# A Strassen-type matmul with GELU: opening in half chunks, block sums put behind the next operand sums, GELU table loaded in front

## Chip, cores, metric

One core of one Trainium2 chip. The metric is device time in microseconds (us) of one execution; the median of several runs is quoted. The runs are compared with runs of the kernel before on the same chip in the same rounds.

## The reference

```python
m, k, n = 4096, 4096, 4096                    # a, b: float32, normal
x = np.matmul(a, b)
return 0.5 * x * (1 + np.tanh(np.sqrt(2 / np.pi) * (x + 0.044715 * x**3)))
```

## The kernel before

The output is made in 16 blocks of 1024 x 1024. Each block takes seven products of half-size matrices instead of eight, with sums of operands (`aS`, `bS`) and sums of results, so 7/8 of the matmuls of a plain product. Operands are loaded as float32 and cast to float16 by the transfer (queue of GpSimd, POOL); A is then transposed by VectorE (DVE). A chunk is 512 x 1024 of A or 1024 x 512 of B, 1.05 MB as float16. The first block does its first half in depth by plain products, which need no sums and few chunks; its second half is done by the seven products, in half as many steps as later blocks have ("half steps"). In the code, X and Y (`accX`, `accY` in the profile) are the running sums of the products in the matmul engine's accumulators; `x1`, `x7` and `m5` are copies of X after three of the products (the prediction's M1 and M5 are among them); `c12` and `c21` are the plain parts of two quadrants of the first block. Near its end the kernel reads a verdict on the size of its inputs, which decides whether another, general path has to run as well; the wait near 1520 us belongs to it.

```python
PLAIN = [   # quadrant of the output, quadrant of A, quadrant of B
    ("12", "11", "12"), ("11", "11", "11"), ("12", "12", "22"), ("11", "12", "21"),
    ("21", "21", "11"), ("21", "22", "21"), ("22", "21", "12"), ("22", "22", "22"),
]
N_PLAIN = 2 * len(PLAIN)
N_WARM = 28                     # matmuls of zeros ahead of the first product
...
def turn_a(mb, quad, c):        # DVE; load_a issues 4 transfers of 256 KB, load_b 8 of 128 KB
    s = staged.pop((mb, quad, c))                 # "stage": two buffers
    t = pool.tile([P, NJ // 2, TM * 2], F16, name="aT", tag=f"aT{a_slot[quad]}{c}")
    ...
    nc.vector.transpose(dst, src)
...
def settle(gi, s, i):           # after the last step of product s, tile i of 4
    X, Y = banks.get(("X", i)), banks.get(("Y", i))
    if s == 1:
        m5 = keep("m5", X, 2)                     # copy on ScalarE (ACT)
        flush()                                   # GELU and output of what waits
        y = new_y()                               # four buffers in all
        tt(y, Y, m5, ALU.subtract)                # on DVE
        if gi == 0:
            tt(y, y, post.pop(("c12", i)), ALU.add)   # the plain part of the first block
        waiting.append((gi, i, 0, 1, y, y))
    elif s == 2:
        post["x7", i] = keep("x7", X, RT)
    elif s == 3:
        x1 = post["x1", i] = keep("x1", X, RT)
        x7 = post["x7", i]
        tt(x7, x1, x7, ALU.subtract)
        tt(x1, Y, x1, ALU.subtract)
        if gi == 0:
            tt(x1, x1, post.pop(("c21", i)), ALU.add)
    ...                         # s = 4: output from X;  s = 5: y = x1 - Y;  s = 6: y = Y + x7
...
for n, whats in (               # ahead of which step: L(oad) A, B and T(ranspose), quadrant_chunk
    (0, "A11_0 B12_0 T11_0 B11_0 A12_0"), (2, "B22_0"), (4, "T12_0 B21_0 A21_0 A22_0"),
    (8, "T21_0 B12_1 B22_1 A11_1"), (10, "T22_0 A12_1"), (14, "T11_1 A22_1 B21_1 B11_1"),
    (16, "T12_1 A21_1"), (18, "T22_1"), (24, "T21_1"),
): ...
for n, step in enumerate(steps):
    ...                         # loads and transposes of this step
    make_sums(...)              # operand sums of step n + 2, on DVE
    flush()
    plain(n) if step[1] < 0 else multiply(*step)
```

Every engine works through its own instructions in this order. What DVE has ahead of a transpose or an operand sum therefore delays it, even where the data are there.

## Time and profile before

| | |
|---|---|
| median of 3 runs | 1596.88 us (1596.72 to 1597.02) |
| span in the profile | 1595.7 us |

The prediction below shows where the time goes, with its lines. The wait for the transposed A21, in the timeline of DVE (start, duration, engine, line, operation, count):

```profile
45.67 0.69 DVE L366 TENSOR_TENSOR x<-x,accX 128x512 f32<-128x512 f32 x1 [0.18 <-PE accX L291]
46.27 4.50 DVE L151 STREAM_TRANSPOSE aT<-stage 128x2048 uint32<-128x2048 uint32 x2
```

The fourth of four additions that wait for PE stands ahead of the transpose, and PE goes on at 48.63 when the first of the two transposes is done.

### The profile page before, as it was taken

What the parts mean: (1) busy time and instruction counts of PE and PEld (TensorE: products, weight loads), DVE (VectorE), ACT (ScalarE), POOL (GpSimd) and SP (SyncE); (2) the same over time, 40 slices, a digit from 0 to 9 for tenths busy, and PEclk for the clock granted to TensorE, in tenths of its full rate; (3) what the DMA queues carried; (4) which work ended last, traced back from release to release, by engine and by line L of the source; (5) the groups of instructions that cost most, each with busy time, mean ns of one, the idle gap of its engine ahead of it and who ended that gap; (6) DMA issues with size and microseconds to landing.
All of it is one profiled execution on the core that took longest, in us unless ns stands there. A gap on an engine that the chain in (4) does not pass through costs nothing. (4 is left out here: it accounts for less than half of the span.)

```text
span 1595.7 us, 19619 instructions
## 1 busy us (share of the span) xinstructions
PE 1568.2 (98%) x7228; PEld 708.3 (44%) x7228; DVE 1229.6 (77%) x1365; ACT 522.5 (33%) x714; POOL 530.9 (33%) x964
## 2 busy tenths in 40 slices
PE   8999999999999999999999999999999999999988
PEld 3444444444444444444444444444444444444433
DVE  1398898867877888985778778887787779888674
ACT  0035545411121545531111344541212145454111
POOL 7563441440323144341124423245021443514300
PEclk9999999999999999999999999999999999999999
DMA  9997683890957578587497837689377786837702
GB/s 179 189 222 149 119 181 74 143 197 27 198 98 147 113 132 158 103 164 130 78 164 118 184 74 147 135 133 178 60 135 129 133 158 106 173 80 136 152 16 81
DMA packets 224792, 211.13 MB, mean 132 GB/s; under 512 B 19888, under 2 KB 191920, under 8 KB 224688
## 3 DMA queue, kind: packets, MB, share of 16 engines
q0 software_dynamic: 187392, 142.67, 60.8%
q1 hardware_dynamic: 37296, 67.13, 11.6%
q8 instruction: 59, 0.97, 0.2%
q14 instruction: 45, 0.37, 0.1%
HBM read 285.22 MB, written 67.11 MB: 221 GB/s over the span
## 5 line engine op out<-in xcount | busy, mean ns | idle before, releaser
L291 PEld LDWEIGHTS <-aS 128*128 128x128 f16 x4960 | 485.6, 98 | 595.9 <-DVE aS L264 7.0
L160 POOL DMA_DIRECT2D bR<-in_b_dram x832 | 448.8, 544 | 709.7 <-DVE bS L264 338.6
L264 DVE TENSOR_TENSOR aS<-aT 128x2048 f16<-128x2048 f16 x310 | 376.0, 1219 | 151.1 <-PE accX L291 117.4
L291 PE MATMUL accX<-bS,aS 128*128 128x512 f16 x1984 | 432.5, 380 | 4.3 <-DVE bS L264 4.1
L264 DVE TENSOR_TENSOR bS<-bR 128x2048 f16<-128x2048 f16 x310 | 375.5, 1218 | 52.5 <-PE accX L291 41.0
L291 PEld LDWEIGHTS <-aT 128*128 128x128 f16 x2240 | 219.6, 98 | 277.7 <-issue 12.4
L357 ACT ACTIVATE y<-y 128x512 f32<-128x512 f32 x192 | 118.7, 630 | 337.9 <-DVE y L366 337.7
L291 PE MATMUL accY<-bR,aS 128*128 128x512 f16 x992 | 216.7, 379 | 3.0 <-DVE aS L264 3.0
L291 PE MATMUL accY<-bS,aS 128*128 128x512 f16 x992 | 216.7, 379 | 1.6 <-DVE y L366 1.6
L291 PE MATMUL accX<-bS,aT 128*128 128x512 f16 x992 | 217.0, 379 | 0.0
L291 PE MATMUL accX<-bR,aS 128*128 128x512 f16 x992 | 216.7, 379 | 0.0
L291 PE MATMUL accY<-bS,aT 128*128 128x512 f16 x992 | 216.7, 379 | 0.0
L366 DVE TENSOR_TENSOR energy<-energy,square 128x1024 bf16<-128x1024 bf16 x240 | 164.6, 686 | 9.3 <-ACT square L185 5.4
L140 POOL DMA_DIRECT2D stage<-in_a_dram x128 | 81.9, 646 | 255.6 <-DVE aT L151 186.5
L344 ACT COPY x<-accX 128x512 f32<-128x512 f32 x128 | 75.1, 587 | 220.0 <-PE accX L291 220.0
L185 ACT ACTIVATE square<-aT 128x1024 bf16<-128x1024 f16 x120 | 123.8, 1051 | 64.9 <-DVE energy L366 64.6
L185 ACT ACTIVATE square<-bR 128x1024 bf16<-128x1024 f16 x120 | 123.5, 1051 | 58.1 <-DVE energy L366 57.4
L151 DVE STREAM_TRANSPOSE aT<-stage 128x2048 uint32<-128x2048 uint32 x32 | 73.7, 2305 | 47.8 <-DMA stage<-in_a_dram 47.8
L344 ACT COPY m<-accX 128x512 f32<-128x512 f32 x64 | 37.1, 580 | 214.4 <-PE accX L291 214.4
L366 DVE TENSOR_TENSOR x<-accX,x 128x512 f32<-128x512 f32 x64 | 43.9, 691 | 41.0 <-ACT y L357 41.0
L357 ACT ACTIVATE y<-accX 128x512 f32<-128x512 f32 x64 | 38.2, 597 | 112.7 <-PE accX L291 112.7
L291 PE MATMUL accY<-bR,aT 128*128 128x512 f16 x192 | 45.4, 398 | 9.7 <-DMA bR<-in_b_dram 6.6
(35 smaller groups left out, 307.9 us busy)
## 6 DMA issues: line engine op xcount, KB each, us to landing
bR<-in_b_dram POOLq DMA_DIRECT2D x832, 128.0 KB, 5.2
out_dram<-y SPq DMA_DIRECT2D x256, 256.0 KB, 5.6
stage<-in_a_dram POOLq DMA_DIRECT2D x128, 256.0 KB, 7.0
row<-seen_d SPq DMA_DIRECT2D x2, 1.5 KB, 3.0
seen_d<-seen SPq DMA_DIRECT2D x1, 3.0 KB, 7.7
```

The costliest lines, as they stand in the source:

```text
L140: nc.gpsimd.dma_start(out=s[g * Q : (g + 1) * Q, :, :], in_=a_v[kh * CH + c, g, :, x0 : x0 + TM // Q, :],)
L151: nc.vector.transpose(dst, src)
L160: nc.gpsimd.dma_start(out=t[g * Q : (g + 1) * Q, e::2, :], in_=b_v[kh * CH + c, g, e, :, :, n0 : n0 + NC],)
L185: nc.scalar.activation(t[:, :], src, ACT.Square)
L264: nc.vector.tensor_tensor(out=t[:, :], in0=part(tiles, blk, o[0], q), in1=part(tiles, blk, o[1], q), op=ALU.add if o[2] > 0 else ALU.subtract,
L291: nc.tensor.matmul(acc[:, :], sa[:, j // 2, i * P : (i + 1) * P, j % 2], sb[:, j, :], start=start and j == 0, stop=stop and j == 3, skip_g ...
L344: nc.scalar.copy(out=t[:, :], in_=src[:, :])
L357: nc.scalar.activation(y[:, :], src[:, :], ACT.Gelu_apprx_tanh)
L366: nc.vector.tensor_tensor(out=o[:, :], in0=x[:, :], in1=y[:, :], op=op)
```

## The change

The intent: begin products with half chunks; keep the matmul engine (PE) warm until then; take additions that nobody waits for out of the way of operand sums; load the GELU table where ACT is idle. Cut to its core:

```diff
-N_WARM = 28
+N_WARM = 44
 def load_a(mb, quad, c, h=None):          # h: half of the rows; 4 transfers of 128 KB each
 def turn_a(mb, quad, c, h=None):          # half a transpose
 def load_b(nb, quad, c, h=None):          # h: even or odd rows in depth
 def plain(n):                             # first four products by halves of B,
                                           # last four by halves of A's rows
 def flush():
     for args in waiting:
+        plain_part = post.pop((f"c{ih + 1}{jh + 1}", i), None) if gi == 0 else None
+        if plain_part is not None:
+            tt(y, y, plain_part, ALU.add)
         emit(*args)
+def combine():                            # called behind make_sums and flush of the next step
+    for gi, i in later:
+        x7, x1 = post["x7", i], post["x1", i]
+        tt(x7, x1, x7, ALU.subtract)
+        tt(x1, banks["Y", i], x1, ALU.subtract)
+    later.clear()
 # settle, s == 1 and s == 5:
-    flush()
+    if gi:
+        flush()
-    if gi == 0:
-        tt(y, y, post.pop(("c12", i)), ALU.add)
 # settle, s == 3:
-    tt(x7, x1, x7, ALU.subtract)
-    tt(x1, Y, x1, ALU.subtract)
-    if gi == 0:
-        tt(x1, x1, post.pop(("c21", i)), ALU.add)
+    later.append((gi, i))
 # loads:
-    (0, "A11_0 B12_0 T11_0 B11_0 A12_0"), (2, "B22_0"), (4, "T12_0 B21_0 A21_0 A22_0"),
+    (0, "A11_0 B12_0 T11_0 B11_0 A12_0 B22_0 B21_0 A21_0"), (4, "T12_0 A22_0"),
-    (24, "T21_1"),
+    (22, "T21_1"),
+table = pool.tile([P, 1], F32, name="table", tag="table")
+nc.vector.memset(table[:, :], 0.0)
+nc.scalar.activation(table[:, :], table[:, :], ACT.Gelu_apprx_tanh)
```

More of the change, by code (lines that the diff above doesn't have):

```diff
@@ L43 @@
 PLAIN = [
-    ("12", "11", "12"), ("11", "11", "11"), ("12", "12", "22"), ("11", "12", "21"),
-    ("21", "21", "11"), ("21", "22", "21"), ("22", "21", "12"), ("22", "22", "22"),
+    ("12", "11", "12", False), ("11", "11", "11", False), ("12", "12", "22", False), ("11", "12", "21", False),
+    ("21", "21", "11", True), ("21", "22", "21", True), ("22", "21", "12", True), ("22", "22", "22", True),
 ]
 N_PLAIN = 2 * len(PLAIN)
-N_WARM = 28
+N_WARM = 44
 SQUARE_MAX = 2.0**26
@@ L132, in half_path, with load_a, turn_a, load_b @@
     staged = {}
-    def load_a(mb, quad, c):
+    def load_a(mb, quad, c, h=None):
         ih, kh = int(quad[0]) - 1, int(quad[1]) - 1
-        x0 = (ih * MH + mb * TM) // Q
-        s = pool.tile([P, TM // Q, RUN], F16, name="stage", tag="stage", bufs=2)
+        n = NX if h is None else NX // 2
+        x = 0 if h is None else h * n
+        x0 = (ih * MH + mb * TM) // Q + x
+        if not h:
+            s = pool.tile([P, NX, RUN], F16, name="stage", tag="stage", bufs=2)
+            staged[mb, quad, c] = s
+        s = staged[mb, quad, c]
         for g in range(4):
             nc.gpsimd.dma_start(
-                out=s[g * Q : (g + 1) * Q, :, :],
-                in_=a_v[kh * CH + c, g, :, x0 : x0 + TM // Q, :],
-            )
-        staged[mb, quad, c] = s
-    def turn_a(mb, quad, c):
-        s = staged.pop((mb, quad, c))
-        t = pool.tile([P, NJ // 2, TM * 2], F16, name="aT", tag=f"aT{a_slot[quad]}{c}")
+                out=s[g * Q : (g + 1) * Q, x : x + n, :],
+                in_=a_v[kh * CH + c, g, :, x0 : x0 + n, :],
+            )
+    def turn_a(mb, quad, c, h=None):
+        if not h:
+            t = pool.tile([P, NJ // 2, TM * 2], F16, name="aT", tag=f"aT{a_slot[quad]}{c}")
+            a_tiles[mb, quad, c] = t
+        s, t = staged[mb, quad, c], a_tiles[mb, quad, c]
+        x = slice(0, NX) if h is None else slice(h * NX // 2, (h + 1) * NX // 2)
         src = s.bitcast(U32).rearrange("p mb (jj q) -> p jj mb q", q=Q)
         dst = t.bitcast(U32).rearrange("p jj (mb q) -> p jj mb q", q=Q)
-        nc.vector.transpose(dst, src)
-        a_tiles[mb, quad, c] = t
-    def load_b(nb, quad, c):
+        nc.vector.transpose(dst[:, :, x, :], src[:, :, x, :])
+        if h != 0:
+            del staged[mb, quad, c]
+    def load_b(nb, quad, c, h=None):
         kh, jh = int(quad[0]) - 1, int(quad[1]) - 1
         n0 = jh * NH + nb * NC
-        t = pool.tile([P, NJ, NC], F16, name="bR", tag=f"bR{b_slot[quad]}{c}")
-        for g in range(4):
-            for e in range(2):
+        if not h:
+            b_tiles[nb, quad, c] = pool.tile(
+                [P, NJ, NC], F16, name="bR", tag=f"bR{b_slot[quad]}{c}"
+            )
+        t = b_tiles[nb, quad, c]
+        for e in range(2) if h is None else (h,):
+            for g in range(4):
                 nc.gpsimd.dma_start(
@@ L163, in load_b @@
                 )
-        b_tiles[nb, quad, c] = t
     def part(tiles, blk, quad, q):
@@ L307, in plain @@
     def plain(n):
-        (quad, oa, ob), q = PLAIN[n // 2], n % 2
+        (quad, oa, ob, by_rows), h = PLAIN[n // 2], n % 2
         chain = "X" if quad == "11" else "Y"
         seen = [x for x in range(len(PLAIN)) if PLAIN[x][0] == quad]
-        start = n == 2 * seen[0]
-        stop = n == 2 * seen[-1] + 1
-        for i in range(RT):
+        sa, sb = a_tiles[0, oa, 0], b_tiles[0, ob, 0]
+        sa = sa.rearrange("p jj (m e) -> p jj m e", e=2)
+        tiles = [(j, e) for j in range(NJ // 2) for e in range(2) if by_rows or e == h]
+        for i in range(h * RT // 2, (h + 1) * RT // 2) if by_rows else range(RT):
             acc = banks[chain, i]
-            products(acc, part(a_tiles, 0, oa, q), part(b_tiles, 0, ob, q), i, start, stop)
+            start = n // 2 == seen[0] and (by_rows or h == 0)
+            stop = n // 2 == seen[-1] and (by_rows or h == 1)
+            for j, e in tiles:
+                nc.tensor.matmul(
+                    acc[:, :], sa[:, j, i * P : (i + 1) * P, e], sb[:, 2 * j + e, :],
+                    start=start and (j, e) == tiles[0], stop=stop and (j, e) == tiles[-1],
+                    skip_group_check=True,
+                )
             if not stop:
@@ L351, in flush @@
         for args in waiting:
+            gi, i, ih, jh, y, _ = args
+            plain_part = post.pop((f"c{ih + 1}{jh + 1}", i), None) if gi == 0 else None
+            if plain_part is not None:
+                tt(y, y, plain_part, ALU.add)
             emit(*args)
         waiting.clear()
+    later = []
+    def combine():
[4 more added lines that the diff above has]
+        later.clear()
     def emit(gi, i, ih, jh, y, src):
@@ L381, in settle @@
         elif s == 3:
-            x1 = post["x1", i] = keep("x1", X, RT)
-            x7 = post["x7", i]
-            tt(x7, x1, x7, ALU.subtract)
-            tt(x1, Y, x1, ALU.subtract)
-            if gi == 0:
-                tt(x1, x1, post.pop(("c21", i)), ALU.add)
+            post["x1", i] = keep("x1", X, RT)
+            later.append((gi, i))
         elif s == 4:
@@ L395, in settle @@
             tt(y, post.pop(("x1", i)), Y, ALU.subtract)
-            flush()
+            if gi:
+                flush()
             waiting.append((gi, i, 1, 0, y, y))
@@ L417, in half_path @@
     for n, whats in (
-        (0, "A11_0 B12_0 T11_0 B11_0 A12_0"),
-        (2, "B22_0"),
-        (4, "T12_0 B21_0 A21_0 A22_0"),
+        (0, "A11_0 B12_0 T11_0 B11_0 A12_0 B22_0 B21_0 A21_0"),
+        (4, "T12_0 A22_0"),
         (8, "T21_0 B12_1 B22_1 A11_1"),
@@ L429, in half_path @@
             fn = {"A": load_a, "B": load_b, "T": turn_a}[what[0]]
-            before.setdefault(n, []).append((fn, (0, what[1:3], int(what[4]))))
+            for h in (0, 1) if what[4] == "0" else (None,):
+                before.setdefault(n, []).append((fn, (0, what[1:3], int(what[4]), h)))
     nxt_b = {"12": "22", "22": "21", "21": "12", "11": "11"}
@@ L507, in half_path @@
             flush()
+            combine()
             if step[1] < 0:
```

## The prediction

> **What bounds the kernel now.** I read the page's totals first, then the busy times by stretch, then the matmul engine's timeline over the first 145 us, then the transfers of the first 60 us, then the waits after 1500 us.
>
> ```profile
> span 1595.7 us, 19619 instructions
> PE 1568.2 (98%) x7228; PEld 708.3 (44%) x7228; DVE 1229.6 (77%) x1365; ACT 522.5 (33%) x714; POOL 530.9 (33%) x964
> ```
>
> Of 7228 matmuls 28 are warm-up, so 7200 are work. The stretches say what one costs and where PE is not full:
>
> ```profile
> core 0: us, PE busy (x) PEld busy (x) DVE busy (x) ACT busy (x) POOL busy (x), PEclk, DMA share, GB/s
> 0.00:20.00 20.00, 12.54 (x42) 4.78 (x43) 2.58 (x2) 1.28 (x1) 14.65 (x29) 0.83 1.06 159
> 40.00:60.00 20.00, 16.93 (x71) 7.20 (x70) 7.17 (x6) 0.00 (x0) 12.74 (x23) 0.91 1.32 196
> 100.00:120.00 20.00, 17.00 (x80) 7.60 (x79) 18.61 (x23) 4.74 (x8) 13.54 (x25) 1.00 1.18 229
> 200.00:400.00 200.00, 200.00 (x928) 90.73 (x927) 159.79 (x184) 71.45 (x96) 58.78 (x107) 1.00 0.64 124
> 1500.00:1560.00 60.00, 55.90 (x253) 24.92 (x252) 38.72 (x55) 10.69 (x19) 0.00 (x0) 0.97 0.07 23
> ```
>
> 928 matmuls in 200 us is 0.2155 us each; 7200 of them are 1551.6 us. So 44 us of the span are lost, and no change that leaves the count alone can gain more. They lie at the two ends: between 140 and 1500 us PE is full. The timeline of PE shows the opening:
>
> ```profile
> 1.31 7.93 PE L303 MATMUL accX<-zeros 128*128 128x512 f16 x28 [1.31 <-DVE zeros L298]
> 15.37 8.69 PE L291 MATMUL accY<-bR,aT 128*128 128x512 f16 x32 [6.12 <-DMA bR<-in_b_dram]
> 31.18 0.38 PE L291 MATMUL accY<-bR,aT 128*128 128x512 f16 x1 [0.21 <-DMA bR<-in_b_dram]
> 38.49 7.07 PE L291 MATMUL accX<-bR,aT 128*128 128x512 f16 x32
> 48.63 29.49 PE L291 MATMUL accY<-bR,aT 128*128 128x512 f16 x128 [3.08 <-DVE aT L151]
> 94.72 11.38 PE L291 MATMUL accX<-bS,aS 128*128 128x512 f16 x52 [0.20 <-ACT m L344]
> 116.02 7.08 PE L291 MATMUL accY<-bR,aS 128*128 128x512 f16 x32 [3.00 <-DVE aS L264]
> 124.68 7.07 PE L291 MATMUL accY<-bS,aS 128*128 128x512 f16 x32 [1.58 <-DVE y L366]
> 131.58 13.76 PE L291 MATMUL accY<-bS,aT 128*128 128x512 f16 x63
> ```
>
> The first block of output ends at 131.58 us after 480 matmuls, 103.4 us of work: 28.1 us are lost. They are: 15.37 before the first product; 1.6 because the first 32 take 8.5 instead of 6.9 us (slow clock); 0.8 on both sides of 31.18; 3.2 before 48.63 and 1.7 of slow clock behind it; 0.4 before 94.72; 3.2 before 116.02; 1.8 before 124.68. At the other end 5.7 us go with the wait at 1524 us (verdict on the inputs, then slow clock) and 7.8 us are the tail after the last matmul. The change touches neither.
>
> The transfers decide what the opening can gain:
>
> ```profile
> DMA  0099999999999999999999999999999999999999
> GB/s 0 3 124 192 153 181 201 202 202 200 202 203 199 188 196 196 201 200 203 199 203 201 212 187 195 196 196 195 195 197 199 202 202 204 202 200 203 197 181 167
> ```
>
> Each slice is 1.5 us. The load queue runs at 200 GB/s without a pause from 8 us on: a chunk of 1.05 MB takes 5.3 us, half a chunk 2.6 us. Nothing in the opening can come sooner than this queue brings it, unless it waits for less of it.
>
> **What the Trainium skill says.** "TensorE: Matmul & The Clock Gate", section "What's actually happening": the array's clock is halved after about 3.4 us of idleness and comes back after as much activity. The trace agrees: after the idle 9.24 to 15.37 and before 48.63 the granted clock falls and matmuls follow each other at 0.43 instead of 0.2155 us; but 3.00 us of idleness before 116.02 cost no clock, so it depends on where the gap lies. "Perfetto Trace Analysis", section "DMA Optimizations": splitting transfers lets work start sooner if the engines are idle; here they are full, so a split buys only the finer granularity. "ScalarE: Activation LUTs", section "What ACT_TABLE_LOAD costs": about 1283 ns plus a drain per switch; the trace has two loads of 1.28 us, one at 0.86 us, one at 90.85 us ahead of the first GELU. "VectorE: DVE Perf Modes", section "The three transpose paths": the DVE transposes 32x32 blocks; here 2.31 us a chunk, so I take 1.15 us for half.
>
> **The change, part by part.** The order of instructions per engine shows that the sequence of chunks in the load queue is unchanged; only the pieces are halves, and the eight loads of a chunk may be the eight outstanding ones.
>
> 1. First product. It waits now for half of A, its transpose, and half of B: three halves ahead of it instead of four. Before, the fourth half let PE start at 15.37; 2.6 us earlier is 12.7. The warm-up, 44 instead of 28, ends at 9.24 + 16 x 0.2155 = 12.7. Both agree; I take 12.8. Gain 2.6, and with no idle gap the 1.6 us of slow clock too: **-4.2**.
>
> 2. Products 3 and 4 of the plain part. PE, 4.2 us ahead, runs out at 12.8 + 64 x 0.2155 = 26.6. The next needs half of B22, whose whole let PE go at 31.2, so its half is there at 28.6 (A12, transposed from 26.58 on, is ready by 27.8). Stall 2.0 where there were 0.8: **+1.2**. From here the queue is no longer ahead of PE by more than half a chunk.
>
> 3. A21. Before, DVE took up its transpose only behind the four additions that wait for PE: PE ended at 45.4, DVE began at 46.27, the transpose of 2.31 ended when PE went on at 48.63. It still stands there, but PE needs half of it: 0.9 + 1.15 = 2.1 us stall instead of 3.2, too short for the slow clock: **-2.8**. Then PE runs to the end of the plain part at 12.8 + 2.0 + 2.1 + 55.2 = 72.1, against 77.96: 5.9 us gained so far.
>
> 4. The half steps behind it (72 to 120 us). Here DVE is full (18.6 of 20 us), so its queue is the path. Per piece from the trace: transpose 2.3, operand sum 1.14, PSUM sum 0.6 to 0.7. Following the new order: T12, two sums, T22, four sums and the four y of M5 end at about 87.5; two sums; the four delayed additions of c12 end at 92.2; two sums; the last transpose runs 94.5 to 96.8 (its data land at 92.7); three sums to 100.2. So the sum before the sixth product is there at 100.2 and needed at 106.5: the 3.2 us wait vanishes, and the copy delayed by the table load (0.4) too: **-3.6**. The eight deferred M1 additions end at 105.5, before PE writes that bank again. But M5's GELUs now wait for the delayed c12, and the four copies behind them on ACT hold PE by some 0.8 us near 93: **+0.8**. DVE then has one sum, four additions, four sums before the y of the seventh product: ready at 114.4 with PE at 114.2; stall 0.2 instead of 1.8: **-1.6**.
>
> 5. The c21 additions go behind that y and the next sum, so GELU starts 3.5 us later relative to PE (118 instead of 114.5), output lands 5.2 to 7.5 us later, and its four buffers hold the next four y, which stand before an operand sum on DVE. Before, that sum was ready 1.9 us early (136.6 against 138.5); now some 1.6 us late: **+1.5**.
>
> 6. In the other 15 blocks the M1 sums move behind an operand sum. PE has no wait there to lose: 0. The table load itself lies beside work in both: 0 more.
>
> Sum: -4.2 + 1.2 - 2.8 - 3.6 + 0.8 - 1.6 + 1.5 = -8.7, so 1596.9 - 8.7 = 1588.2; I say **1588**.
>
> **Rivals.** (a) The load queue takes everything back: PE gets ahead and meets it at each chunk. For it: 200 GB/s without a pause, and step 2 is such a wait. Against: the chunks behind A22 were there before PE needed them by 5 us and more, as no wait of PE names a transfer after 31.8 us. If true, gain 4 us, 1593. (b) DVE takes it back: the half steps hold 54 us of its work in 48 us of PE's. For it: its 93% share; steps 4 and 5 are already this. If another 2 us stall of step 2 or 3 grows to 3 and halves the clock: +1.5 to +3, 1590 to 1591. (c) No rest remains: outputs land at once, the stalls of steps 4 and 5 vanish, 1585.5. (d) The deferred sums disturb the steady part: 15 blocks at 0.3 us would be 4.5 us; against it, DVE is idle 20% there and PE never waited.
>
> **Range and chances.** The terms of 1, 3 and 4 are sure in kind; each is uncertain by half a microsecond to one, the waits added in 2, 4 and 5 by one to two, and the slow clock comes in lumps of 1.5. Together that is about 3 us: 1585 to 1591.5. Two per cent is 32 us, more than all that is lost outside of the start and tail, so "faster" and "slower" are nearly excluded.
>
> **What would show it.** Right: first product at 12.5 to 13.2 at full clock; a wait for bR of about 2 near 28; a wait for aT of about 2 near 44; no wait for aS near 110; the first block ending near 121; a short wait for bS near 129; PE full from 140 to 1490; the wait near 1510 as before. Wrong: half loads that slow the queue below 190 GB/s, slow clock in the opening, or any PE wait in the steady part.

## The result

| | before | changed |
|---|---|---|
| median of 6 runs, us | 1596.80 (1596.34 to 1598.43) | 1591.68 (1590.89 to 1594.28) |
| span in the profile, us | 1595.7 | 1589.5 |

The ratio of the times is 0.9969, with a 95% interval of 0.9956 to 0.9982. A gain of some 5 us, then, where 8.7 was predicted, and 0.2 us outside of the range.

The changed kernel's page and PE's timeline, to be held against the lines of before in the prediction:

```profile
span 1589.5 us, 19678 instructions
PE 1570.7 (99%) x7244; PEld 710.1 (45%) x7244; DVE 1229.0 (77%) x1370; ACT 520.9 (33%) x714; POOL 539.1 (34%) x980
```

```profile
1.31 12.39 PE L315 MATMUL accX<-zeros 128*128 128x512 f16 x44 [1.31 <-DVE table L531]
13.72 7.07 PE L332 MATMUL accY<-bR,aT 128*128 128x512 f16 x32
20.62 7.07 PE L332 MATMUL accX<-bR,aT 128*128 128x512 f16 x32
30.31 8.75 PE L332 MATMUL accY<-bR,aT 128*128 128x512 f16 x32 [2.62 <-DMA bR<-in_b_dram]
38.90 7.07 PE L332 MATMUL accX<-bR,aT 128*128 128x512 f16 x32
47.98 27.80 PE L332 MATMUL accY<-bR,aT 128*128 128x512 f16 x128 [2.01 <-DVE aT L159]
...
97.00 7.07 PE L303 MATMUL accX<-bS,aS 128*128 128x512 f16 x32 [0.51 <-DVE aS L276]
...
110.81 7.07 PE L303 MATMUL accY<-bR,aS 128*128 128x512 f16 x32
117.72 7.07 PE L303 MATMUL accY<-bS,aS 128*128 128x512 f16 x32
124.63 7.07 PE L303 MATMUL accY<-bS,aT 128*128 128x512 f16 x32
133.47 7.07 PE L303 MATMUL accY<-bS,aT 128*128 128x512 f16 x32 [1.77 <-DVE bS L276]
140.37 13.98 PE L303 MATMUL accX<-bR,aS 128*128 128x512 f16 x64
```

Every start minus the start before it, minus the count times 0.2155, is time lost. The waits near 110 and 117 us are gone, as intended. The start came 1.65 us earlier and warm (another 1.6). But PE then waits 2.8 us for the fifth chunk (27.52 to 30.31), and the 32 matmuls behind it take 8.59 instead of 6.90 us. Behind the first block there is a new wait of 1.9 us ahead of 133.47. The first block ends at 124.63 instead of 131.58, and 64 matmuls later (140.37 against 145.37, which is 131.58 plus 64 matmuls at 0.2155 us) the gain is 5.0 us. The 6.2 us between the two spans have 1.2 more, from the end (0.4 at the wait near 1515 us, 0.6 in the tail, 0.3 between, rounded), which no part of the change explains; I count it as difference between runs.

The new wait at 133 us shows in DVE's timeline of the changed kernel: the first of the last four results of the block waits for a buffer, that is for an output to land, and the operand sum that PE needs stands behind all four:

```profile
127.45 0.69 DVE L400 TENSOR_TENSOR y<-accY,x 128x512 f32<-128x512 f32 x1 [3.18 <-DMA out_dram<-y]
...
132.20 1.22 DVE L276 TENSOR_TENSOR bS<-bR 128x2048 f16<-128x2048 f16 x1
```

### The slow clock

PE's clock in the changed kernel, in stretches of 3.41 us (columns: stretch, its length, busy time and count of PE, of weight loads, DVE, ACT, POOL, then the granted clock, the DMA share and GB/s):

```profile
27.33:30.74 3.41, 0.79 (x5) 0.23 (x3) 1.25 (x1) 0.00 (x0) 2.98 (x6) 1.00 1.23 199
30.74:34.16 3.42, 3.42 (x10) 1.21 (x9) 0.00 (x0) 0.00 (x0) 2.65 (x6) 0.50 1.18 187
44.40:47.81 3.41, 1.57 (x8) 0.49 (x5) 3.06 (x4) 0.00 (x0) 2.81 (x6) 1.00 1.45 195
47.81:51.22 3.41, 3.25 (x15) 1.48 (x16) 3.41 (x4) 0.00 (x0) 2.75 (x6) 1.00 1.25 202
```

Slow stretches begin and end on a grid of 3.41 us, whose position against the kernel's start differs from profile to profile. In the first pair PE idled most of a window and the next window ran at half clock, ten matmuls instead of sixteen. In the second it idled 2.0 us in its window and the clock stayed. The same kernel, profiled once more (a0 below), idles 2.2 us at the same place inside one window of its grid, and loses the clock:

```profile
45.42:48.84 3.42, 1.41 (x8) 0.47 (x6) 3.07 (x5) 0.00 (x0) 2.81 (x6) 1.00 1.42 193
48.84:52.25 3.41, 3.41 (x10) 1.23 (x9) 3.03 (x3) 0.00 (x0) 2.78 (x6) 0.50 1.24 202
```

I laid the grid over all 14 profiles and took PE's idle time in each window from the starts of the matmuls. (The first 7 us are left out: matmuls begin 0.43 us apart there, up to 6.8 us in the changed kernel, but the record of the clock shows 1.00.) Every window with up to 2.03 us of idleness left the clock full; every one with 2.07 us and more halved it in the next window. (Two windows with 1.05 and 1.42 us that were themselves slow prolonged the slow stretch.) The gap between the two sides is as small as the error of this working: worked out anew, the 2.03 came out as 2.05. So the limit lies near 2.05 us, no more exactly than that. The closest on either side, and those of the text:

| profile | window, us | idle in it | clock in the next |
|---|---|---|---|
| before | 114.05 to 117.46 | 1.98 | full |
| changed | 44.40 to 47.81 | 2.01 | full |
| e2 (tail) | 1584.93 to 1588.34 | 2.03 | full |
| e7 | 133.28 to 136.69 | 2.07 | half |
| e1 | 43.50 to 46.92 | 2.18 | half |
| changed, again (a0) | 45.42 to 48.84 | 2.19 | half |
| changed | 27.33 to 30.74 | 2.78 | half |
| before | 45.78 to 49.20 | 2.86 | half |

A window at half clock costs half of 3.41 us, 1.7 us. This is one reason why runs of the same kernel differ: the six runs of the changed kernel took 1590.9 to 1591.8 at a mean clock of 0.997, 1592.7 at 0.995 and 1594.3 at 0.994. It is not the only one: the five runs of e9 took 1590.6 to 1593.7 us, all at 0.997.

### The profile page after: what moved, and what is told of

Its sections match the earlier page's. It is cut to its first block, busy times and chain, and to the rows that moved or that the text cites. A ratio compares the mean times of both kernels' runs of the same rounds, so it can differ in the third digit from the quotient of the medians.

```text
span 1589.5 us, 19678 instructions
## 1 busy us (share of the span) xinstructions
PE 1570.7 (99%) x7244; PEld 710.1 (45%) x7244; DVE 1229.0 (77%) x1370; ACT 520.9 (33%) x714; POOL 539.1 (34%) x980
## 5 line engine op out<-in xcount | busy, mean ns | idle before, releaser
L303 PEld LDWEIGHTS <-aT 128*128 128x128 f16 x1984 | 194.2, 98 | 236.0 <-issue 2.1
L146 POOL DMA_DIRECT2D stage<-in_a_dram x144 | 90.0, 631 | 247.4 <-DVE aT L159 180.4
L159 DVE STREAM_TRANSPOSE aT<-stage 128x2048 uint32<-128x2048 uint32 (+1 forms) x36 | 74.2, 2068 | 43.7 <-DMA stage<-in_a_dram 43.6
L400 DVE TENSOR_TENSOR y<-accY,m 128x512 f32<-128x512 f32 x64 | 42.6, 688 | 13.5 <-ACT m L364 13.3
```

What stands on the lines that cost most here:

```text
L146: nc.gpsimd.dma_start(out=s[g * Q : (g + 1) * Q, x : x + n, :], in_=a_v[kh * CH + c, g, :, x0 : x0 + n, :],)
L159: nc.vector.transpose(dst[:, :, x, :], src[:, :, x, :])
L303: nc.tensor.matmul(acc[:, :], sa[:, j // 2, i * P : (i + 1) * P, j % 2], sb[:, j, :], start=start and j == 0, stop=stop and j == 3, skip_g ...
L400: nc.vector.tensor_tensor(out=o[:, :], in0=x[:, :], in1=y[:, :], op=op)
```

## The experiments

Twelve kernels ran, all with correct results, five rounds each.

| run | median, us | before on that chip | ratio (95%) |
|---|---|---|---|
| a0 changed, again | 1593.02 | 1597.29 | 0.9970 (0.9957 to 0.9984) |
| e1 opening only | 1593.54 | 1597.29 | 0.9975 (0.9962 to 0.9989) |
| e2 sums only | 1595.18 | 1597.29 | 0.9986 (0.9972 to 1.0000) |
| e3 one wait filled | 1592.15 | 1597.29 | 0.9973 (0.9960 to 0.9987) |
| e4 results in place | 1588.07 | 1598.37 | 0.9937 (0.9923 to 0.9951) |
| e5 A21 turned earlier | 1593.15 | 1598.37 | 0.9969 (0.9956 to 0.9983) |
| e9 A loaded whole | 1591.35 | 1598.37 | 0.9957 (0.9944 to 0.9971) |
| e8 e3 + e4 + e5 | 1587.89 | 1598.37 | 0.9937 (0.9924 to 0.9951) |
| e12 three waits filled | 1590.25 | 1598.15 | 0.9953 (0.9940 to 0.9965) |
| e6 28 warm-up matmuls | 1594.23 | 1598.15 | 0.9971 (0.9957 to 0.9986) |
| e7 no early table load | 1592.83 | 1598.15 | 0.9965 (0.9953 to 0.9977) |
| e10 best version | 1582.25 | 1598.15 | 0.9907 (0.9893 to 0.9920) |

An interval is about 4 us wide, so differences of 2 us between two of these are not told by the times; where I rely on less, it is on the profile.

**a0: the changed kernel again.**

> The changed kernel once more, as the reference for the other runs on this chip. Expected 0.9969 of the kernel before, some 1591.5 us. Theory (clock): its runs differ by whole steps of 1.7 us, because each 3.4 us stretch at half clock costs 1.7 us and their number differs from run to run; the granted clock should fall with the time, about 0.001 per 1.7 us. Rival (transfers differ from run to run): times vary at the same granted clock.

Same ratio. The profile has three slow windows before 1500 us (behind the fifth chunk, A21 and the operand sum at 136 us) where the first had one; its span is 5 us longer at a clock of 0.995. Its five times grow as the clock falls, as the clock theory has it (1591.2 us at 0.997 to 1596.2 at 0.995), but three slow windows instead of one are 3.4 of the 5 us; the first product at 14.27 against 13.72 us shows that the transfers vary too, by half a microsecond.

**e1 and e2: each half of the change alone.** e1 is the changed kernel with `flush`, `settle` and `T21_1` as before and without the table; e2 is the kernel before with the changed `flush`, `combine`, `settle` and `T21_1`.

> Only the opening: half chunks, half products, 44 warm-up matmuls; the sums on DVE, the last transpose and the table load as before. My account of the traces: the earlier first product is given back at the fifth chunk, so the plain part ends at 75.6 instead of 77.96 us, and the later waits (3.2 and 1.8 us) stay: gain 2.4 us, 1594.5. The prediction's own step sum for these parts was 5.8 us, 1591.

> Only the order of the sums: M1 sums behind the next operand sums, c12 and c21 additions delayed, last transpose two steps up; opening and table load as before. Account of the traces: 4.6 us gained before the seventh product, 1.9 lost at the wait for buffers behind it: 1594 us, gain 2.5 to 3. If instead the half opening is what made room on DVE, the waits near 116 and 124 us stay and the gain is below 1 us.

e1: the plain part ended at 75.52 us, and the waits of 3.2 and 1.8 us behind it were there as before. e2: they were gone, PE ran 106.82 to 127.54 us without one, and the wait for the new buffers cost 1.7 us at 136.16. Both as expected. So the two halves work on different parts of the opening, and the second needs nothing of the first. What the halves are worth in time (4.0 and 2.2 us by the ratios, with such intervals) can't be separated better; e1's median lies between its two forecasts, and e2's gain just under its own.

**e3 and e12: is it the wait or the clock behind it?** Both let PE multiply zeros while it waits, into running sums (which adds nothing) or into a bank that is cleared next.

```diff
+if n == 4:  fill(banks["X", RT - 1], 12, False)     # e3 and e12: before the fifth chunk
+if n == 8:  fill(banks["Y", RT - 1], 9, True)       # e12: before A21
+if n == 32: fill(banks["Y", RT - 1], 9, False)      # e12: before the operand sum of block 2
```

> The changed kernel with 12 matmuls of zeros (2.6 us) added into the running sum of one bank while PE waits for the fifth chunk. If the slow clock behind that wait is what the prediction missed, the 32 matmuls behind it take 6.9 instead of 8.6 us, PE still starts them at about 30.3, and the run is 1.7 us shorter than the changed kernel. If the transfers set the pace there anyway (rival), the time gained is waited for at the next chunks: the wait for the transposed A21 grows by 1.7 us and the run stays the same.

e3: the fifth chunk's products started at 30.52 us and took 6.91 us, as the clock theory has it, and the wait for A21 did not grow (2.2 us). But in this profile the slow window fell behind A21 instead, and the time stayed. So the experiment told the clock from the transfers, and that one wait filled is not enough.

> The changed kernel with every wait left where it is, but three of them (fifth chunk, A21, operand sum of the second block) filled with 12, 9 and 9 matmuls of zeros that take no longer than the wait. Tells slow clock from waiting. If the slow clock is what the prediction missed: no slow stretch before 1500 us, the three waits end where they did, and the run is 1.7 to 3.4 us below the changed kernel, 1588 to 1590. If the waits alone are the cost, it equals the changed kernel, 1591 to 1593.

PE's timeline of e12:

```profile
27.41 2.75 PE L311 MATMUL accX<-own_zeros 128*128 128x512 f16 x12
30.27 7.07 PE L339 MATMUL accY<-bR,aT 128*128 128x512 f16 x32
...
44.08 2.11 PE L311 MATMUL accY<-own_zeros 128*128 128x512 f16 x9
46.25 27.80 PE L339 MATMUL accY<-bR,aT 128*128 128x512 f16 x128
...
96.08 7.07 PE L303 MATMUL accX<-bS,aS 128*128 128x512 f16 x32 [1.30 <-ACT x L371]
...
130.61 2.11 PE L311 MATMUL accY<-own_zeros 128*128 128x512 f16 x9
132.81 7.07 PE L303 MATMUL accY<-bS,aT 128*128 128x512 f16 x32
```

All three waits are as long as they were (2.9, 2.2 and 2.2 us), no window before 1500 us is slow, and the 128 matmuls from 46.25 take 27.64 us. Median 1590.25, 2.6 us below e7, which ran in the same rounds and differs from the changed kernel by the table alone. It is just above the expected range, and the two intervals overlap, so the size is not told by the times. (By the spans, e12 gains 0.9 us on the first profile of the changed kernel: one slow window less, 1.7, and 0.8 us more lost before 96.08, where a copy by ACT came last.) That the clock behind these waits costs time, and not the waits alone, is shown by the profiles.

**e4: results in place.**

```diff
 elif s == 6:
-    y = new_y()
-    tt(y, Y, post.pop(("x7", i)), ALU.add)
+    x7 = post.pop(("x7", i))
+    y = new_y() if gi else x7
+    tt(y, Y, x7, ALU.add)
```

> The changed kernel, but the last four results of the first block are written over their own operand tiles and not into the four y buffers, so they wait for no output to land. Theory (buffers held by the delayed GELU): the wait of PE for an operand sum in the first steps of the second block, 1.9 to 2.6 us in the profiles so far, goes, and with it a chance of slow clock: 2 to 3 us less than the changed kernel. Rival (that operand sum waits for its own transfer or for DVE's other work): the wait stays above 1 us.

The wait is gone: PE starts 64 matmuls at 124.41 and the next at 138.22, without a pause. The ratio falls to 0.9937, outside of the changed kernel's interval: some 5 us by the ratios, 3.6 to 5 by the medians, more than expected. The wait (1.9 to 2.6 us, 3.7 in e6) brought a slow window behind it in five of the seven profiles that had it in this opening (a0, e5, e6, e7, e9; not in the first of the changed kernel and in e3), so some 4 us, 5.4 in e6, is what those could lose.

**e5: A21 turned earlier.**

```diff
-(8, "T21_0 B12_1 B22_1 A11_1"),
+(7, "T21_0"), (8, "B12_1 B22_1 A11_1"),
```

> The changed kernel with the two half transposes of A21 one half step earlier in DVE's order, ahead of the four additions that wait for PE. Theory (the order on DVE makes that wait, the data are there at 42.9 us): the wait of 2.2 us before the fifth product goes, and so does its chance of slow clock (1.7 us, seen in three of the four profiles of this opening that were taken later): 2 to 4 us less. Rival (transfers set the pace of the opening, so PE meets them at the next chunk): the wait turns up again before A22, by more than 1 us, and the time stays.

The wait for A21 went, as the theory said: PE goes on at 45.75 without a pause. But the time did not change. The gain was given back later, at a place that neither theory named: DVE waits for a chunk of B, the second of B21, and PE for the operand sum behind it. From PE's timeline and DVE's of e5:

```profile
45.75 27.79 PE L332 MATMUL accY<-bR,aT 128*128 128x512 f16 x128
...
96.37 7.07 PE L303 MATMUL accX<-bS,aS 128*128 128x512 f16 x32 [1.79 <-DVE aS L276]
```

```profile
84.41 1.23 DVE L276 TENSOR_TENSOR bS<-bR 128x2048 f16<-128x2048 f16 x1 [2.05 <-DMA bR<-in_b_dram]
```

The first block ends at 124.00 against 124.63 us. The rival was right that the transfers take it back, and wrong about where.

**e9: A loaded whole.** `load_a` issues its four transfers of 256 KB at once; transposes and products stay in halves.

> The changed kernel with the A chunks loaded whole again (four transfers of 256 KB instead of eight of 128 KB), still turned and multiplied in halves. In the profiles the queue moved 0.16 MB less in the first 12 us with half loads, and the first product came at 13.7 to 14.4 us instead of the 12.8 predicted. If half loads slow the start of the queue: first product at 12.8 to 13.3, the fifth chunk 0.6 to 0.9 us earlier, run up to 1 us shorter. If the whole A makes the first half of it late (rival): first product later than 13.7 and no gain.

First product at 14.07 us, the fifth chunk's at 30.95: no earlier, as the rival had it, since the first half of A was turned only by 12.70 instead of 9.32 us. The fourth piece of the first B landed at 13.9, no earlier than with half loads of A (13.6). So nothing here shows that smaller transfers made the start later than predicted. The time is not told apart from the changed kernel's.

**e6: 28 warm-up matmuls.** `N_WARM = 28`.

> The changed kernel with 28 warm-up matmuls as before. They end near 9.2 us, PE then idles over 4 us until the first product at about 13.7 us. Expected: slow clock for 8 to 16 products, 1.7 to 3.4 us of matmul time; but the plain part is held by the fifth chunk at 30.1 us, where PE waits 2.4 to 2.8 us, so that wait shrinks by as much: PE's start of the fifth chunk moves by under 1 us and the run stays within 1 us of the changed kernel. If warm clock at the start matters for the end, it is 1.7 to 3.4 us longer.

```profile
13.56 8.49 PE L332 MATMUL accY<-bR,aT 128*128 128x512 f16 x32 [3.62 <-DMA bR<-in_b_dram]
...
29.41 7.07 PE L332 MATMUL accY<-bR,aT 128*128 128x512 f16 x32 [0.45 <-DMA bR<-in_b_dram]
```

The first 32 matmuls take 8.33 us, so the slow start costs 1.4 us; but PE then waits 0.6 instead of 2.8 us for the fifth chunk, which came 0.9 us earlier in this run than in the first profile of the changed kernel (for a likely reason see "The halves" below). The longer warm-up, by itself, buys nothing that these runs tell: what it gains is waited for 14 us later. The ratio is the changed kernel's.

**e7: no early table load.** The three lines of the table removed.

> The changed kernel without the early GELU table load. The load of 1.28 us then stands before the first GELU near 94 us, and the copies of X behind it on ACT come 1.3 us later, about 97.7 instead of 96.4: PE waits near 97 for a copy, 0.7 to 1.3 us more than the 0.66 of the changed kernel. So 0.5 to 1.3 us longer. If the copy has slack there: no difference.

No difference in PE's waits there (98.63 us starts after 0.67 us lost, as in the changed kernel); my first expectation was a miss. ACT's timeline says why: the load lies in time in which ACT waits for DVE anyway.

```profile
92.05 1.28 ACT L391 ACT_TABLE_LOAD   x1
95.67 2.44 ACT L391 ACTIVATE y<-y 128x512 f32<-128x512 f32 x4 [2.33 <-DVE y L400]
```

**e8: the three edits together.** 12 zero matmuls as in e3, results in place, A21 earlier.

> The changed kernel with all three: 12 zero matmuls in the wait for the fifth chunk, A21's transposes one half step earlier, results in place. Expected: no slow clock before 1500 us, first block ending near 120.5 instead of 124.6, no wait of PE over 1 us behind it, and 5 to 7 us less than the changed kernel: 1585 to 1587. If the transfers take it back, at least one wait for a transfer of over 1 us appears between 45 and 110 us and the run is not under 1589.

1587.89, a miss of the expectation by about 1 us: no slow clock before 1500 us, but PE loses 0.7 us before 87.81 and 2.0 us before 94.95, behind the same chunk of B as in e5, and the block ends at 122.57 instead of 120.5. By its time it is no better than e4; by its profile it is 1.8 us ahead of e4 at the second product of the second block (150.20 against 152.03).

**e10: the best version.** e8, with half of B21's second chunk loaded ahead of A22's second chunk, and the verdict on the inputs fetched one product earlier in the last block:

```diff
-(10, "T22_0 A12_1"),
-(14, "T11_1 A22_1 B21_1 B11_1"),
+(10, "T22_0 A12_1 B21_1a"),              # a, b: halves
+(14, "T11_1 A22_1 B21_1b B11_1"),
...
+at(len(groups) - 1, 1, 0, lambda: fetch(said["seen"]))   # the two transfers of the verdict
 at(len(groups) - 1, 2, 0, answer)                        # DVE's part, as before
```

> The version with the three edits of the run before, half of B21's second chunk loaded ahead of A22's second chunk (the queue has a gap there, since A22 waits for a stage buffer), and the inputs' verdict fetched one product earlier in the last block. Expected: DVE's wait of 2.3 us for B21 near 81 us shrinks to under 1; PE's waits of 0.6 and 1.8 us near 87 and 94 us shrink to under 1 together; the wait of 3.4 us before 1515 us goes, and with it its slow clock in most runs. In all 4 to 6 us below the version with three edits: 1581 to 1584. If the verdict's fetch is not what DVE waits for there, the wait near 1515 stays above 2 us.

```profile
93.60 7.07 PE L308 MATMUL accX<-bS,aS 128*128 128x512 f16 x32 [1.30 <-DVE aS L281]
...
1510.15 20.88 PE L308 MATMUL accX<-bS,aS 128*128 128x512 f16 x96 [0.53 <-DVE bS L281]
```

1582.25 us, ratio 0.9907: faster than both kernels, its interval lies below both of theirs. DVE's wait for B21 is gone, one of 1.2 us for A22 has come, and PE loses 1.5 us before 93.60 (expected under 1). The wait near 1515 us fell from 3.5 to 0.5, and no slow window stands behind it. (Nor did one in e8's profile, where that wait was split 1.9 and 1.7 between two windows.) That last edit belongs to no part of the change; it is in because that wait was the largest left.

## Why the prediction was wrong

Of its mechanism, the waits held: each that it named was found, removed or made where it said. Its rule for the clock and its times of landing did not, and its sum was off by 3.7 us. The terms by the two profiles:

| step of the prediction | predicted | measured | told by |
|---|---|---|---|
| 1 first product earlier, and warm | -4.2 | -3.3 | start 13.72, not 12.8 |
| 2 wait for the fifth chunk | +1.2 | +2.0 | 2.8 us instead of 0.8 |
| 2 slow clock behind that wait | 0 | +1.7 | window from 30.74 us; e3, e12 |
| 3 wait for A21, its slow clock | -2.8 | -2.8 | 2.2 instead of 3.2 us |
| 4 half steps | -4.4 | -4.6 | no wait near 110 and 117 us; e2 |
| 5 buffers held by the late GELU | +1.5 | +1.9 | e4 |
| 6 steady part | 0 | 0 | PE full from 140 to 1490 us |
| sum | -8.7 | -5.1 | timeline at 140 us: -5.0; medians: -5.1 |

**The clock.** The step that failed most is the clause of step 3, "2.1 us stall instead of 3.2, too short for the slow clock", and the zero for the clock behind step 2's stall of 2.0 us. I had one wait of 3.00 us that cost no clock (before 116.02) and concluded that shorter ones are safe. That wait was spread over two windows, 1.2 and 1.98 us. What counts is the idle time inside one window: 2.03 us was safe, 2.07 was not, so a wait of 2.8 us is hit unless a window ends near its middle. The wait for A21 was spared in the first profile, so step 3 looks right by its number, but in four of the eight profiles with this wait unfilled (a0, e1, e3, e7) it cost 1.7 us. The prediction's second rival, "grows to 3 and halves the clock", is the course that the run took, with the threshold put at 3 us where it is 2.

**The halves.** Steps 1 and 2 took the moment at which PE began (15.37 and 31.2 us) for the moment at which the whole chunk was there, and took one half, 2.6 us, off. But PE begins with the even rows of B. The profile of before had the answer, in the transfers by issue and landing: the eighth piece of the first B was issued at 11.01 and landed 4.9 us later, at 15.9; the fourth was issued at 5.72 and landed 7.6 us later, at 13.3. The changed kernel's fourth piece was issued at 8.23 and landed 5.3 us later, at 13.6, and the product began at 13.72. These are the first B's pieces of the changed kernel (the five issued up to 8.9 us):

```profile
L173 POOL DMA_DIRECT2D bR<-in_b_dram x5: 544/544/556, 6.1 to 8.9; - x5
DMA to landing us min/median/max: 5.3/5.5/5.6
```

So the queue kept its pace up to there, and 0.6 us of the 0.9 are this misreading. In this profile the warm-up would have held PE as well: 13 of its matmuls came 0.43 us apart, where 7 did before, so that it ended at 13.5 and not at step 1's 12.7. But in e8 it ended at 12.6 and the product still began at 13.55, so the half chunk decides.

At the fifth chunk the same slip is some 0.5 us (the eighth piece of B22, issued at 26.75, landed 4.9 us later, at 31.7, so a half 2.6 us earlier is there at 29.1, not at 28.6). In e6 the fourth piece landed at 29.3; in the changed kernel it was issued at 24.4 and landed at 30.2. For this other 1 us the traces have a likely cause. Beside the loads the DMA engines carry a packet of 16 KB, 0.96 us long, in a queue that the profile calls "instruction". In the changed kernel it falls between 24.5 and 27.5 us (columns: packets, MB, share of 16 engines):

```profile
q8 instruction: 1, 0.02, 2.0%
```

One piece of A then in flight landed 6.3 us after its issue, those before it 5.1, and the pieces behind were later too. In the eleven profiles with 44 warm-up matmuls the packet came at 25 to 26 us, and B22's fourth piece landed 16.1 to 16.9 us after the first B's (15.8 in e1 alone); in the three with 28 (before, e2, e6) it came at 33 to 35 us, and the distance was 15.8. So it seems that the longer warm-up itself brought the packet in front of the fifth chunk. No run tests this alone, so the cause of this 1 us is not shown.

**Worth of the warm-up.** Of the 3.3 us of step 1, the 1.6 of the warm clock are real in PE's timeline, but e6 does not show them worth anything at the end: without them PE waits that much less for the fifth chunk.

**Right for the wrong reason.** The 0.4 us before 94.72 were put down to the table load. In the trace of before it ended at 92.13 us, and the GELU behind it had to wait for DVE's addition until 92.21 anyway. This GELU stood between the copies of M5 in ACT's order; the changed order puts the four copies first, and e2, without the early load, loses the wait as well. And the 0.7 us before 97.00 are there as predicted, 0.8, but an operand sum came last, not a copy.

## What to carry to other kernels

Before an earlier start is counted as a gain, follow the queue to the next place where PE meets it: there the gain is waited for, as here at the fifth chunk. Price a wait of PE not by its length alone: lay the clock's windows over it, and fill waits of 2 us and more with harmless matmuls or split them. And when work of a side engine is put off, look for what it holds in the meantime: here four output buffers, which came back as a wait of 2 us and a slow window.

## What the Trainium skill lacked or had wrong

- "TensorE: Matmul & The Clock Gate", section "Why this matters for your kernels", advises no idle gaps of PE over about 3 us. The grid of windows of 3.41 us that the page describes was found here. But the limit is lower: 2.07 us of idleness in one window halved the clock in the next (e7), 2.03 to 2.05 us did not (e2), in 14 profiles without an exception, and a gap of 3.2 us that was split 1.2 and 1.98 between two windows cost none (before).
- "DMA: Bandwidth & Descriptors", section "Anatomy of one DMA — SWDGE (gpsimd) path", fits 2.0 us plus bytes over 436e3 for a transfer; an estimate from it is 2.3 us for 128 KB. In the full queue of this opening, with up to eight transfers outstanding, a piece of 128 KB landed 4.5 to 7.7 us after its issue. The page has no word on the time to landing when the queue is full, which is what the opening of a kernel needs. An estimate from this case comes out right: eight pieces, 1.05 MB, at 200 GB/s take 5.2 us.
